# A transformer layer on one core: parameter loads, zero stores, the last head's output and the w_ada sums moved between stages

## The chip, the cores and the metric

The kernel runs on one core of a Trainium2 chip. The metric is the device time of one execution in microseconds (us). Five engines work side by side, each on its own queue in order: PE (matmuls), VectorE (DVE in the profile), ScalarE (ACT), GpSimd (POOL) and SP, which here only issues DMAs.

## The reference

One layer over 1024 latent tokens (plus 256 context tokens), all in float32, D = 1024:

```python
mod = silu(c) @ w_ada + b_ada                 # six vectors: shift, scale, gate, twice
h   = modulate(rmsnorm(x), sh1, sc1)          # context likewise, with c_ctx
q, k, v, z, xbc, dt_raw, gates = split(h @ w_in)
o   = differential attention, 8 heads, softmax(q1 k1) - lam * softmax(q2 k2), then rmsnorm per head
dt  = softplus(dt_raw + dt_bias); a = -exp(a_log)
y   = bidirectional state-space scan of silu(conv(xbc)) with dt, a  + d_skip * x
mix = (sigmoid(g_a) * (o @ w_branch_attn) + sigmoid(g_s) * (norm(y * silu(z)) @ w_branch_ssd)) @ w_out
x   = x + gt1 * rmsnorm(mix)
h   = modulate(rmsnorm(x), sh2, sc2)
f   = shared expert(h) + sum over the 8 chosen of 64 experts
out = x + gt2 * rmsnorm(f)
```

## The kernel before

The program is one class, `Layer`, whose stages follow one another: `norm_and_qkv`, `mixer_t`, `attention`, `merge_and_out`, `moe`, `final`. A product of two float32 matrices is made from three matmuls of high and low parts (`mm3`, L418): each operand is split on the way in, `hi` by a ScalarE copy and `lo` by a VectorE subtraction.

The order on PE, VectorE, ScalarE and GpSimd is written by a planner, `Flow` (L106). Each piece of work is a generator (a stream) that yields what it needs next: tiles, free buffers of a `Ring`, times, or an engine. `Flow.run` (L331) keeps a clock per engine from modelled durations and always continues the stream that can go first, the lowest priority number first; the instruction is emitted at that place. Where a yield holds a number, the stream goes on no earlier than that modelled time. On the chip the four engines then run their lists in that order, each waiting for its data. SP's list is not among those: `run` (L2420) hands only four engines over for a schedule by hand, and the framework orders SP's issues itself.

The places that the change touches:

- `ada_late` (L1508) computes 4096 of the modulation's columns while the q, k and v blocks run. For each of 32 columns of 128, a 512-KB chunk of w_ada comes into one of two `wada` buffers, VectorE sums its eight rows of c-weighted values into a `wacc` accumulator (L1538 to 1540), and PE adds over the partitions with a product with ones into the bank `adab` (L1545). One stream does the columns one after the other; two accumulators take turns.
- `mixer_ahead` (L763) opens the pool `tw` with the mixer's weight buffers during the last q block and starts the load of the dt weights. `mixer_t` (L784) loads `dcol` (d_skip) and `db` (dt_bias, a_log) at L813 to 818, in the pool `sp`, whose memory the buffers of the q, k and v blocks held before. `dt_post` (L826) is the first to need `db`: ScalarE takes its exponential, copies the three banks of dt products into `G` buffers (a ring of two), and PE folds them with 20 small matmuls.
- `branches` (L1194) multiplies the scan's and then the attention's output with their branch weights: four passes, (ssd, 0), (ssd, 1), (attn, 0), (attn, 1), each over half of the tokens, with 8 rows of outputs of 24 matmuls. `operands` (L1225) loads eight operands per pass, each 256 KB read back from DRAM, into `bxh` and `bxl`, rings of eight pairs, which one pass fills wholly: a pair comes free while the last row of the pass runs. All loads of this stage share four `braw` buffers.
- `norm` (L1470) in `attention` scales a finished head in the SBUF tile `ot` and stores it to DRAM (`oT`). Attention ends in the planner when eight heads are counted (L1505), and only then does the program go on to `merge_and_out`.
- `merge_and_out` (L1578) first fills a tile with zeros and stores it 16 times (256 KB each) over `yacc[1]` (L1603), to which half of the experts' outputs are added later; then w_out's 16 loads come as a stream of low priority (L1607). The output projection `main` (L1632) runs over eight tiles of 128 tokens, 48 matmuls each.

Of the kernel before, what the change touches and what calls it, by code (L numbers as in the profile page):

```python
# [9 lines left out]
F32 = mybir.dt.float32  # L10
# [364 lines left out]
class Layer:  # L375
# [387 lines left out]
    def mixer_ahead(s):  # L763

        F = s.F
        wp = s.open("tw")
        s.mw = raws, his, los = s.ring(wp, [P, KC, P], "raw", 2), s.ring(wp, [P, KC, P], "hi", 2, F32R), s.ring(wp, [P, KC, P], "lo", 2, F32R)
        s.zgs = s.ring(wp, [P, 512], "zg", 2)
        s.mbox = []
        F.spawn(0, s.mixer_load(COL_DT, 32, s.mbox))  # L770

    def mixer_load(s, c0, n, box):
# [11 lines left out]
    def mixer_t(s):  # L784
# [10 lines left out]
        if True:  # L795
# [14 lines left out]
            Rs = s.ring(sp, [P, 512], "R", 6)  # L810
            Gs = s.ring(sp, [P, 4, P], "G", 2)
            Ws = s.ring(sp, [P, 4, P], "W", 2)
            dcol = mp.tile([P, 8], F32, name="dcol")  # L813
            for q in range(2):
                F.dma(dcol[64 * q:64 * q + 64], bass.AP(tensor=I["d_skip"].tensor, offset=q, ap=[[0, 64], [2, 8]]))
            db = mp.tile([P, 2, 32], F32, name="db")
            F.dma(db[:, 0], s.brow("dt_bias", 0, 32))
            F.dma(db[:, 1], s.brow("a_log", 0, 32))
            dtn = mp.tile([P, 2, 10, 32], F32, name="dtn")
            dt, dtd = dtn[:, 0], dtn[:, 1]  # L820
            ac = mp.tile([P, 2, 10, 16], F32, name="ac")
# [372 lines left out]
    def branches(s):  # L1194


        F, I = s.F, s.I
        op, pp = s.open("fl", side="right"), s.open("fps", True, side="right")
        s.ysg = [s.dram(f"ysg{m}", [P, T]) for m in range(8)]
        s.oT = [s.dram(f"oT{h}", [P, T]) for h in range(8)]  # L1200
        s.acc = acc = s.ring(pp, [P, 512], "bacc", 2)
        s.raws = raws = s.ring(op, [P, 512], "braw", 4)
        xhs, xls = s.ring(op, [P, 512], "bxh", 8, F32R), s.ring(op, [P, 512], "bxl", 8, F32R)
        whs, wls = s.ring(op, [P, 4, P], "bwh", 3, F32R), s.ring(op, [P, 4, P], "bwl", 3, F32R)
        s.bxs = xs = {}
        ws = {}
        s.st = st = {"heads": 0, "pairs": 0, "merged": 0, "mg": None}
        todo = [("ssd", 0), ("ssd", 1), ("attn", 0), ("attn", 1)]

        def half(raw, hi, lo, then, first=False):  # L1210
            yield [raw, "ACT"]
            F.acopy(hi, raw)
            if first:
                yield [hi, "POOL"]
                F.ptt(lo, raw, hi.bitcast(F32), ALU.subtract)
            elif 0 < st["pairs"] < 32:
                yield [hi, "DVE"]
                F.tt(lo, raw, hi.bitcast(F32), ALU.subtract)
            else:
                yield [hi, "DVE|POOL"]  # L1220
                F.sub(lo, raw, hi.bitcast(F32))
            raws.put(raw)
            then()

        def operands():  # L1225
            for kind, h in todo:
                for k in range(8):
                    src = (s.yn if kind == "ssd" else s.oT)[k]
                    yield [raws, xhs, xls, "NOW"] + ([lambda: st["heads"] > k, src] if kind == "attn" else [])
                    raw, hi, lo = raws.get(), xhs.get(), xls.get()  # L1230
                    F.dma(raw, src[:, h * 512:h * 512 + 512])
                    F.spawn(3, half(raw, hi, lo, lambda q=(kind, h, k), v=(hi, lo): xs.update({q: v}), (kind, h, k) == todo[0] + (4,)))

        def weights():
            for kind, h in todo:
                wb = I["w_branch_" + kind][0].rearrange("(k p) c -> p k c", p=P)
                for m in range(8):
                    for a in range(2):
                        yield [raws, whs, wls, "NOW"]
                        raw, hi, lo = raws.get(), whs.get(), wls.get()  # L1240
                        rv = raw.rearrange("p (k c) -> p k c", k=4)
                        F.dma(rv, wb[:, 4 * a:4 * a + 4, m * P:(m + 1) * P])
                        F.spawn(3, half(rv, hi, lo, lambda q=(kind, h, m, a), v=(hi, lo): ws.update({q: v})))

        def main():
            for n, (kind, h) in enumerate(todo):
                for m in range(8):
                    if kind == "ssd":
                        yield [lambda: st["pairs"] >= PACE[8 * n + m]]
                    yield [acc]  # L1250
                    b = acc.get()
                    for k in range(KC):
                        yield [lambda: (kind, h, k) in xs and (kind, h, m, k // 4) in ws]
                        (xh, xl), (wh, wl) = xs[kind, h, k], ws[kind, h, m, k // 4]
                        yield [xh, F.ready[_n(xl)] + SLACK[5], wh, wl]
                        s.mm3(b, wh[:, k % 4], wl[:, k % 4], xh, xl, k == 0, k == KC - 1)
                        if k % 4 == 3:
                            whs.put(wh)
                            wls.put(wl)
                        if m == 7:  # L1260
                            xhs.put(xh)
                            xls.put(xl)
                    F.spawn(3, (gated if kind == "ssd" else merge)(h, m, b))

        def gated(h, m, b):
            sl = slice(h * 512, h * 512 + 512)
            yield [raws, "NOW"]
            g = raws.get()
            F.dma(g, s.gt[8 + m][:, sl])
            yield [g, b, "DVE"]  # L1270
            F.tt(g, b, g, ALU.mult)
            acc.put(b)
            F.dma(s.ysg[m][:, sl], g)
            raws.put(g)

        def merge(h, m, b):
            sl = slice(h * 512, h * 512 + 512)
            yield [lambda: st["mg"] is not None]
            ys, gs = st["mg"]
            yield [ys, gs, "NOW"]  # L1280
            y, g = ys.get(), gs.get()
            F.dma(g, s.gt[m][:, sl])
            F.dma(y, s.ysg[m][:, sl])
            yield [g, b, "DVE"]
            F.tt(g, b, g, ALU.mult)
            acc.put(b)
            yield [y, g, "DVE|POOL"]
            F.either(y, y, g, ALU.add)
            gs.put(g)
            yield [y, "ACT"]  # L1290
            hi, lo = s.mh[m, h], s.ml[m, h]
            F.acopy(hi, y)
            yield [hi, "DVE|POOL"]
            F.sub(lo, y, hi.bitcast(F32))
            ys.put(y)
            st["merged"] += 1

        F.spawn(3, weights())
        F.spawn(3, operands())
        F.spawn(4, main())  # L1300

# [37 lines left out]
    def attention(s):  # L1339
        tc, nc, F = s.tc, s.nc, s.F  # L1340
        ap, pp = s.open("at"), s.open("aps", True)
        if True:
# [127 lines left out]
            def norm(h, ot, s0):  # L1470
# [18 lines left out]
                for half in range(2):  # L1489
                    sl = slice(half * 512, half * 512 + 512)  # L1490
                    yield [F.ready[_n(r)] + SLACK[3], acc]
                    pb = acc.get()
                    for i in range(4):
                        F.tp(pb[:, i * P:(i + 1) * P], r[:, 4 * half + i:4 * half + i + 1].to_broadcast([P, P]), s.ident)
                    yield [pb, "DVE"]
                    F.stt(ot[:, sl], ot[:, sl], s.gsub, pb, ALU.mult, ALU.mult)
                    acc.put(pb)
                s0s.put(s0)
                F.dma(s.oT[h], ot)
                ots.put(ot)  # L1500
# [7 lines left out]
    def ada_late(s, pool, pm):  # L1508
# [3 lines left out]
        s.adar = s.dram("adar", [32, P])  # L1512
        wada = I["w_ada"][0].rearrange("(p k) c -> p k c", p=P)
        ws = s.ring(pool, [P, KC, P], "wada", 2)
        accs = s.ring(pool, [P, P], "wacc", 2)
        v = pool.tile([56, P], F32, name="lrows")
        F.dma(v[:32], bass.AP(tensor=I["b_ada"].tensor, offset=2048, ap=[[P, 32], [1, P]]))
        for i, n in enumerate(("g_post_mix", "g_pre_ffn", "g_post_ffn")):
# [5 lines left out]
        def loads():  # L1524
            for j in range(32):
# [3 lines left out]
                F.dma(w, wada[:, :, c0:c0 + P])  # L1529
                got.append(w)  # L1530

        F.spawn(0, loads())
        for j in range(32):
            yield [lambda: len(got) > 0]
            w = got.pop(0)
            yield [w, accs, "DVE"]
            acc = accs.get()
            F.ts(acc, w[:, 0], s.cc[:, 0, 0:1], None, ALU.mult)  # L1538
            for k in range(1, KC):
                F.stt(acc, w[:, k], s.cc[:, k, 0:1], acc, ALU.mult, ALU.add)  # L1540
                if k == 3:
                    yield ["DVE"]
            ws.put(w)
            yield [acc]
            F.mm(pm[:, j:j + 1], acc, s.ones[:, :1], True, True)  # L1545
            accs.put(acc)
        yield [v]
        F.tp(pm[:, 64:120], v, s.ident[:56, :56])
        yield [pm, "DVE"]
        F.vcopy(col, pm[:, 64:120])  # L1550
# [27 lines left out]
    def merge_and_out(s):  # L1578
# [21 lines left out]
        got = []  # L1600
        zero = pg.tile([P, 512], F32, name="zero")
        F.fill(zero, 0.0)
        for t in range(8):  # L1603
            for h in range(2):
                F.dma(s.yacc[1][t * P:(t + 1) * P, h * 512:(h + 1) * 512], zero)

        def weights():  # L1607
            for k in range(8):
# [23 lines left out]
        def main():  # L1632
            for t in range(8):
                tok = slice((t % 4) * P, (t % 4 + 1) * P)
                acc = accs[t % 2]
                yield [(acc, 2)]
                banks = [acc.get(), acc.get()]
                for k in range(KC):
# [825 lines left out]
```

## Time and profile before

| | us |
|---|---|
| median of three runs | 2836.93 |
| lowest and highest run | 2828.54, 2843.67 |
| the profiled execution | 2838.21 |
| its span, first to last instruction | 2836.1 |

| engine | busy us | share of the span |
|---|---|---|
| PE | 2624.0 | 93% |
| VectorE | 2000.2 | 71% |
| ScalarE | 1339.9 | 47% |
| GpSimd | 882.9 | 31% |

The shares are averages over stages with different limits, so they are read stage by stage: the q, k and v blocks end near 411 us, the mixer near 1050, attention near 1523, the merge and output projection near 1780, and the experts fill the rest up to the final 56 us. The mean granted clock of PE was 0.967 of the full 2.4 GHz. A row's "[idle before <- releaser]" is how long that engine stood before the instruction and what let it go; L163 is ScalarE's copy, L170 VectorE's two-tensor operation, L147 the matmul, L211 any DMA issued by SP.

### The profile page before, as it was taken

Reading aid. Unit: us, or ns where it says so; the run is one execution under the profiler, and the core shown is the slowest. Engines: PE = TensorE matmul, PEld = TensorE weight load, DVE = VectorE, ACT = ScalarE, POOL = GpSimd, SP = SyncE. Lnnn points to the kernel's source line nnn. Section 1 sums busy time; section 2 is a strip of 40 time slices with the busy share of each in tenths; the row PEclk is TensorE's granted clock in tenths of the full one; section 3 lists DMA queues with packets and bytes.
Section 4 is the critical chain, followed back from the end, with each engine's and each line's share of the span. In section 5 each row is a group of like instructions: output and inputs, shape, how many; then the busy total and the mean of one; then the engine's idle time right before and its main releaser. Section 6 shows DMA issues by size and latency. Waiting matters only on the chain. (4 is left out here: it accounts for less than half of the span.)

```text
span 2836.1 us, 41280 instructions
## 1 busy us (share of the span) xinstructions
PE 2624.0 (93%) x14561; PEld 2109.4 (74%) x14561; DVE 2000.2 (71%) x4690; ACT 1339.9 (47%) x2105; POOL 882.9 (31%) x670
## 2 busy tenths in 40 slices
PE   7999979999999999999998899899999998999991
PEld 4777868878787776888887687678887776777660
DVE  6876123577776658888893657867788877787863
ACT  4211113344444445666673422335666656576641
POOL 0101010444454520000000000056656656666641
PEclk9999989999999999999999999999999999999995
DMA  7667242243424345224234853478899998999997
GB/s 278 211 205 201 84 127 84 75 130 93 134 82 138 101 133 183 88 84 145 92 101 152 266 164 109 184 247 250 278 310 302 316 302 266 308 305 312 327 306 212
DMA packets 275266, 544.89 MB, mean 192 GB/s; under 512 B 31546, under 2 KB 166819, under 8 KB 248050
## 3 DMA queue, kind: packets, MB, share of 16 engines
q1 hardware_dynamic: 238898, 435.31, 45.1%
q0 software_dynamic: 36160, 106.93, 14.8%
q8 instruction: 115, 1.88, 0.3%
q14 instruction: 93, 0.76, 0.1%
HBM read 432.99 MB, written 124.73 MB: 197 GB/s over the span
## 5 line engine op out<-in xcount | busy, mean ns | idle before, releaser
L170 DVE TENSOR_TENSOR gl<-raw,gh 128x1024 fp32r<-128x1024 f32 x240 | 288.3, 1218 | 40.4 <-ACT gh L163 40.2
L147 PE MATMUL acc<-hh,hi 128*128 128x512 f32 (+2 forms) x760 | 303.7, 400 | 1.4 <-DVE ux L186 1.4
L163 ACT CAST gh<-raw 128x1024 fp32r<-128x1024 f32 x240 | 247.6, 1051 | 101.2 <-PE gu L147 65.9
L147 PE MATMUL acc<-hl,hi 128*128 128x512 f32 (+2 forms) x760 | 287.8, 379 | 0.0
L147 PE MATMUL gu<-gh,xh 128*128 128x512 f32 (+3 forms) x672 | 280.7, 418 | 3.8 <-ACT xh L163 3.4
L147 PE MATMUL acc<-hh,lo 128*128 128x512 f32 (+1 forms) x736 | 279.3, 380 | 2.5 <-DVE lo L170 2.5
L147 PE MATMUL gu<-gl,xh 128*128 128x512 f32 (+3 forms) x672 | 266.7, 397 | 4.4 <-DVE gl L170 4.3
L147 PE MATMUL gu<-gh,xl 128*128 128x512 f32 (+3 forms) x672 | 266.9, 397 | 3.8 <-DVE xl L170 3.7
L261 POOL DMA_INDIRECT cr<-cumd,crow x98 | 124.8, 1273 | 440.7 <-DVE y L197 408.8
L192 DVE TENSOR_SCALAR_CACHE_REDUCE e<-sps 128x512 f32<-128x512 f32 (+1 forms) x384 | 214.2, 596 | 31.2 <-PE sps L147 31.0
L267 POOL DMA_INDIRECT yacc<-y,tk x98 | 180.4, 1841 | 86.3 <-issue 31.3
L147 PE MATMUL sps<-qk 128*128 128x512 f32 (+1 forms) x768 | 195.4, 385 | 8.2 <-DVE e L192 4.5
L155 ACT ACTIVATE e<-e,st 128x1280 f32<-128x1280 f32 x128 | 174.7, 1366 | 31.2 <-DVE st L201 31.0
L147 PE MATMUL acc<-hi,hh 128*128 128x512 f32 x448 | 183.3, 409 | 0.0
L261 POOL DMA_INDIRECT wc<-wtab,tk x98 | 137.9, 1407 | 141.3 <-DVE tk L181 93.9
L147 PE MATMUL acc<-hi,hl 128*128 128x512 f32 x448 | 177.3, 396 | 0.4 <-DVE hl L170 0.4
L147 PE MATMUL acc<-lo,hh 128*128 128x512 f32 x448 | 177.1, 395 | 0.0
L147 PEld LDWEIGHTS sps<-qk 128*128 128x128 f32 x768 | 140.0, 190 | 41.7 <-DVE e L192 10.8
L147 PEld LDWEIGHTS acc<-hh,hi 128*128 128x128 f32 (+1 forms) x760 | 143.5, 189 | 31.2 <-issue 3.7
L147 PE MATMUL pv<-wr,vv 128*128 128x256 f32 x640 | 164.2, 380 | 0.0
L147 PEld LDWEIGHTS acc<-hl,hi 128*128 128x128 f32 (+1 forms) x760 | 143.7, 189 | 25.3 <-issue 0.6
L147 PEld LDWEIGHTS acc<-hh,lo 128*128 128x128 f32 x736 | 139.6, 190 | 29.7 <-DVE lo L170 3.0
(323 smaller groups left out, 6253.7 us busy)
## 6 DMA issues: line engine op xcount, KB each, us to landing
raw<-in_w_e_gate_dram SPq DMA_DIRECT2D x64, 1024.0 KB, 10.6
raw<-in_w_e_up_dram SPq DMA_DIRECT2D x64, 1024.0 KB, 11.3
draw<-in_w_e_down_dram SPq DMA_DIRECT2D x64, 1024.0 KB, 10.0
qk<-qk POOLq DMA_DIRECT2D x16, 1664.0 KB, 8.4
raw<-in_w_in_dram SPq DMA_DIRECT2D x40, 512.0 KB, 4.6
wada<-in_w_ada_dram SPq DMA_DIRECT2D x32, 512.0 KB, 5.2
R<-acd SPq DMA_DIRECT2D x64, 256.0 KB, 5.4
qk<-sa SPq DMA_DIRECT2D x52, 256.0 KB, 4.3
```

What stands on the lines that cost most here:

```text
L147: s.nc.tensor.matmul(out, l, r, start=start, stop=stop)
L155: s.nc.scalar.activation(out, in_, fn, **kw)
L163: s.nc.scalar.copy(out, in_)
L170: s.nc.vector.tensor_tensor(out, a, b, op=op)
L192: s.nc.vector.tensor_scalar(out, a, s1, None, op0=op0, op1=op1, accum_out=acc)
L261: s.nc.gpsimd.indirect_dma_start(out=out, out_offset=None, in_=table, in_offset=bass.IndirectOffsetOnAxis(ap=idx, axis=0), **kw)
L267: s.nc.gpsimd.indirect_dma_start(out=table, out_offset=bass.IndirectOffsetOnAxis(ap=idx, axis=0), in_=in_, in_offset=None, compute_op=ALU. ...
```

## The change

Four edits, all of order and place; no product or sum is added or left out.

1. `dcol` and `db` become tiles of the pool `tw`, and their four loads are issued in `mixer_ahead`, before the load of the dt weights.
2. In `ada_late` a column's VectorE work is planned 4 us after its chunk is expected, and its matmul becomes a stream of its own, planned 4 us after the sum is expected; four accumulators instead of two.
3. The 16 zero stores are emitted in the output projection's loop, two in front of each tile's matmuls.
4. The first half of head 7's output is split from SBUF inside `norm`, into a pair of `branches`' rings, and `operands` no longer loads it.

```diff
@@ mixer_ahead
+        s.dcol, s.db = wp.tile([P, 8], F32, name="dcol"), wp.tile([P, 2, 32], F32, name="db")
+        F.dma(s.db[:, 0], s.brow("dt_bias", 0, 32))
+        F.dma(s.db[:, 1], s.brow("a_log", 0, 32))
+        for q in range(2):
+            F.dma(s.dcol[64 * q:64 * q + 64], bass.AP(tensor=s.I["d_skip"].tensor, offset=q, ap=[[0, 64], [2, 8]]))
         F.spawn(0, s.mixer_load(COL_DT, 32, s.mbox))
@@ mixer_t
-            dcol = mp.tile([P, 8], F32, name="dcol")
-            for q in range(2):
-                F.dma(dcol[64 * q:64 * q + 64], bass.AP(tensor=I["d_skip"].tensor, offset=q, ap=[[0, 64], [2, 8]]))
-            db = mp.tile([P, 2, 32], F32, name="db")
-            F.dma(db[:, 0], s.brow("dt_bias", 0, 32))
-            F.dma(db[:, 1], s.brow("a_log", 0, 32))
+            dcol, db = s.dcol, s.db
@@ branches, operands
+                    if (kind, h, k) == ("attn", 0, 7):
+                        yield [lambda: ("attn", 0, 7) in xs]
+                        continue
@@ attention, norm
                     acc.put(pb)
+                    if (h, half) == (7, 0):
+                        yield [*s.bx, ot, "ACT"]
+                        hi, lo = (q.get() for q in s.bx)
+                        F.acopy(hi, ot[:, sl])
+                        yield [hi, "DVE"]
+                        F.tt(lo, ot[:, sl], hi.bitcast(F32), ALU.subtract)
+                        s.bxs["attn", 0, 7] = hi, lo
@@ ada_late
-        accs = s.ring(pool, [P, P], "wacc", 2)
+        accs = s.ring(pool, [P, P], "wacc", 4)
+        def column(j, acc):
+            yield [F.ready[_n(acc)] + 4000.0]
+            F.mm(pm[:, j:j + 1], acc, s.ones[:, :1], True, True)
+            accs.put(acc)
+            done.append(j)
-            yield [w, accs, "DVE"]
+            yield [F.ready[_n(w)] + 4000.0, accs, "DVE"]
             ws.put(w)
-            yield [acc]
-            F.mm(pm[:, j:j + 1], acc, s.ones[:, :1], True, True)
-            accs.put(acc)
-        yield [v]
+            F.spawn(0, column(j, acc))
+        yield [v, lambda: len(done) == 32]
@@ merge_and_out
-        for t in range(8):
-            for h in range(2):
-                F.dma(s.yacc[1][t * P:(t + 1) * P, h * 512:(h + 1) * 512], zero)
             for t in range(8):
                 tok = slice((t % 4) * P, (t % 4 + 1) * P)
                 acc = accs[t % 2]
+                for h in range(2):
+                    F.dma(s.yacc[1][tok.start + t // 4 * 512:tok.stop + t // 4 * 512, h * 512:(h + 1) * 512], zero)
                 yield [(acc, 2)]
```

## Rows read from the trace of the kernel before

**Rows 1.** Stretches (us): PE, PEld, DVE, ACT, POOL busy, clock, DMA share, GB/s

```profile
60.00:260.00 200.00, 189.93 (x890) 155.12 (x891) 161.83 (x372) 40.45 (x58) 25.23 (x18) 0.97 0.70 208
...
411.50:424.00 12.50, 0.04 (x1) 0.04 (x1) 0.00 (x0) 0.79 (x3) 0.00 (x0) 0.60 0.19 40
...
435.00:1050.00 615.00, 588.53 (x3358) 491.41 (x3357) 407.84 (x962) 260.50 (x373) 244.12 (x208) 0.98 0.35 106
...
1544.80:1555.80 11.00, 0.00 (x0) 0.00 (x0) 0.00 (x1) 0.62 (x1) 0.00 (x0) 0.61 1.03 356
...
1555.80:1582.00 26.20, 21.13 (x67) 14.38 (x68) 14.46 (x22) 11.15 (x18) 0.00 (x0) 0.84 0.80 252
...
1582.00:1620.00 38.00, 38.00 (x169) 31.32 (x167) 30.50 (x48) 18.74 (x32) 0.00 (x0) 1.00 0.86 271
...
1664.00:1770.00 106.00, 106.00 (x527) 85.54 (x526) 69.23 (x208) 26.77 (x61) 0.00 (x0) 1.00 0.32 112
...
1770.00:2780.00 1010.00, 955.16 (x5813) 732.79 (x5812) 785.42 (x1516) 582.60 (x912) 566.98 (x392) 0.98 0.88 285
```

**Rows 2.** Waits of PE, 0 to 410 us: total, times, longest

```profile
PE adab L147 <- DVE wacc L186: 7.9, 3, 4.7
```

**Rows 3.** Timeline of PE, 140 to 158: start, length, operation [idle before]

```profile
149.70 0.59 PE L147 MATMUL adab<-cst,wacc 128*128 128x1 f32 x2 [4.66 <-DVE wacc L186]
...
150.15 0.77 PE L147 MATMUL acc<-hi,hh 128*128 128x512 f32 x1
...
154.13 0.56 PE L147 MATMUL acc<-hi,hh 128*128 128x512 f32 x1
```

**Rows 4.** Timeline of VectorE (DVE), 136 to 158

```profile
146.64 0.29 DVE L179 TENSOR_SCALAR wacc<-wada,cc 128x128 f32<-128x128 f32 x1 [6.70 <-DMA wada<-in_w_ada_dram]
```

**Rows 5.** Timeline of SP's DMA issues, 285 to 500

```profile
345.35 4.34 SPq L211 DMA_DIRECT2D raw<-in_w_in_dram  x3
...
405.00 3.79 SPq L211 DMA_DIRECT2D qk<-sb  x4
...
409.99 1.78 SPq L211 DMA_DIRECT2D dcol<-in_d_skip_dram  x2
...
412.76 0.43 SPq L211 DMA_DIRECT2D db<-in_a_log_dram  x1
```

**Rows 6.** Timeline of ScalarE (ACT), 335 to 432

```profile
423.21 0.23 ACT L155 ACTIVATE db<-db 128x32 f32<-128x32 f32 x1 [19.21 <-DMA db<-in_a_log_dram]
```

**Rows 7.** Timeline of PE, 424 to 437

```profile
423.96 4.47 PE L147 MATMUL aux<-fold,G 64*128 64x32 f32 x20 [12.48 <-ACT G L163]
...
428.37 0.79 PE L147 MATMUL acc<-hh,hi 128*128 128x512 f32 x1
...
434.08 0.54 PE L147 MATMUL acc<-hl,hi 128*128 128x512 f32 x1
```

**Rows 8.** Timeline of SP's DMA issues, 1470 to 1660

```profile
1540.49 9.39 SPq L211 DMA_DIRECT2D yacc<-zero  x13
...
1550.68 0.58 SPq L211 DMA_DIRECT2D braw<-in_w_branch_ssd_dram  x1
...
1630.24 0.33 SPq L211 DMA_DIRECT2D braw<-in_w_out_dram  x1
```

**Rows 9.** Timeline of PE, 1544 to 1572

```profile
1555.82 0.80 PE L147 MATMUL bacc<-bxh,bwh 128*128 128x512 f32 x1 [11.03 <-ACT bwh L163]
...
1560.25 0.63 PE L147 MATMUL bacc<-bxl,bwh 128*128 128x512 f32 x1
...
1570.15 0.50 PE L147 MATMUL bacc<-bxh,bwh 128*128 128x512 f32 x1 [2.84 <-ACT bxh L163]
```

**Rows 10.** Stretch 415 to 417, columns as in rows 1

```profile
415.00:417.00 2.00, 0.00 (x0) 0.00 (x0) 0.00 (x0) 0.00 (x0) 0.00 (x0) 0.50 0.05 0
```

**Rows 11.** Tile wacc: lengths in ns, first and last start

```profile
L179 DVE TENSOR_SCALAR wacc<-wada,cc x32: 273/285/1320, 84.0 to 247.2; 128x128 f32<-128x128 f32 x32
```

**Rows 12.** Tile woh: lengths in ns, first and last start

```profile
L147 PE MATMUL gu<-woh,mh x64: 389/389/499, 1669.0 to 1761.6; 128*128 128x512 f32 x64
```

More of the change, by code (lines that the diff above doesn't have):

```diff
@@ L1202, in branches @@
         s.raws = raws = s.ring(op, [P, 512], "braw", 4)
-        xhs, xls = s.ring(op, [P, 512], "bxh", 8, F32R), s.ring(op, [P, 512], "bxl", 8, F32R)
+        s.bx = xhs, xls = s.ring(op, [P, 512], "bxh", 8, F32R), s.ring(op, [P, 512], "bxl", 8, F32R)
         whs, wls = s.ring(op, [P, 4, P], "bwh", 3, F32R), s.ring(op, [P, 4, P], "bwl", 3, F32R)
@@ L1530, in loads @@
                 got.append(w)
+        def column(j, acc):
[3 more added lines that the diff above has]
+            done.append(j)
+        done = []
         F.spawn(0, loads())
```

## The prediction

> **What bounds the kernel now.** I read the stretches first [rows 1]: PE's busy time, its granted clock and the DMA share, stage by stage. PE is busy over 94% of the long stretches, in one fixed order of instructions. So the kernel is as long as PE's work plus PE's gaps, and a gap that closes moves everything behind it forward. Three dents are to be seen: 60 to 260 us (189.93 busy of 200), 411.5 to 424 (0.04 of 12.5) and 1544.8 to 1555.8 (nothing of 11, while the DMA share is 1.03). I then asked for PE's waits and followed each dent back on the engine that released it.
>
> The first dent: PE waited three times, 7.9 us in all, for the w_ada sums `wacc` [rows 2], the longest 4.66 us [rows 3]. VectorE itself had stood 6.70 us for the chunk `wada` from DMA [rows 4]. A late load blocks VectorE's queue, and VectorE's late sum blocks PE's.
>
> The second dent: SP issued `dcol` and `db` at 410 to 413 us, behind the last `qk` stores [rows 5]. ScalarE stood 19.21 us until `db` had landed [rows 6]. Its next instructions are the copies of the dt banks, PE's fold matmuls need these and waited 12.48 us, and the first conv matmuls stand behind the folds in PE's order [rows 7].
>
> The third: SP issued 13 of the 16 zero stores from 1540.49 on, one per 9.39/13 = 0.72 us, and the next chunk of w_branch_ssd only at 1550.68 [rows 8]. PE waited 11.03 us for its split [rows 9].
>
> Each dent also drops the clock to the lower level (1.2 GHz): the 14 matmuls from 428.37 to 434.08 stand 0.44 us apart [rows 7], against 38.00/169 = 0.225 at the full level [rows 1]. A slow matmul costs about 0.21 us more.
>
> **1, parameters ahead.** Nothing is added; four issues move from 410 to about 345 us, beside the first mixer weights (the three `raw` loads at 345.35 [rows 5]). Gone: the 12.48 us wait; 14 x 0.21 = 3.0 us of slow conv matmuls; and about half of the 4.47 us of folds, 2.2 us, an estimate from the two clock levels. Kept: the third dt copy, which needs a G buffer back from PE; 1 us is my estimate, from its neighbours' lengths. Sum 16.7, taken as 16. Bounds 12 (the wait alone) to 17.7. Where it shifts, the dt chain and all loads tied to it shift along; the mixer's PE (588.53 of 615 busy) has 4% of waits that move as they are.
>
> The cost at the new place: SP spends some 3 us on four issues. Behind them stands the load of the dt weights, wanted by PE only after the last `qk` block, whose stores run to 405 [rows 5]. At 415 to 417 us the DMA share was 0.05 with nothing else running [rows 10]: the scattered parameters went through about one engine of 16 (0.8 of one) until 423. So up to 10 us of one engine now lie ahead of a share of the dt weights, and ScalarE, which splits them, can stand for as long. PE's cover is the accumulator ring of four banks, some 5 us of matmuls each (24 x 0.225). I take 0; with the cover gone it is 10 us once.
> The Trainium skill would price this differently ("DMA: Bandwidth & Descriptors", the section on why a DMA increments its semaphore by 16): the engine count is the largest divisor up to 16 of the slowest dimension, which for 64 partitions means all 16 engines. By that rule the 10 us bound would be under 1 us. The row speaks for one engine, and the bound stays at 10.
>
> **2, w_ada's sums.** The instructions stay; the planner now places VectorE's chain 4 us after it thinks the chunk landed and PE's matmul 4 us after it thinks the sum is done, with four accumulators instead of two. Against the late load of 6.70 us there are 8 us in series for PE. Gone: 7.9 us of waits; after the longest, ten matmuls from 150.15 to 154.13 were slow [rows 3], 2.1 us, and the other waits' share goes by their length, 2.1 x 3.2/4.66 = 1.4. Sum 11.4; taken as 10, since VectorE's 4 us cover less than 6.70 and what stands behind it there are the rope steps that PE needs. Bounds 4.7 (the longest wait alone) to 11.4. Later sums cost nothing: the last started at 247 us [rows 11], and only the end of the `qk` blocks near 400 waits for them. Even 4 us on each of 32 columns, unhidden, ends at 247 + 128 = 375.
>
> **3, zeros and the last head.** Gone from the dent: 11.03 us, and eleven slow matmuls (1555.82 to 1560.25 [rows 9]) x 0.21 = 2.3; 13.3 in all. SP issues the same 16 stores later. In the out-projection (1664 to 1770) the share is 0.32 and 16 x 0.72 = 11.5 us of transfers would hide. But does SP leave them there? Its queue is not written by hand, the other engines' are. The loads of conv weights come from a later stage of the program than the `qk` stores, and the trace has them before those stores (345.35 against 405.00 [rows 5]): what has its data and its memory ready goes up. A zero store needs only the memset. So it probably leaves soon after it, between the loads of the merge, where the share is 0.80 and then 0.86 [rows 1]. There 26.2 x 0.20 + 38 x 0.14 = 10.6 us are free over 64 us: hidden only if the stores are spread. Bounds: 0 kept (a block of 11.5 us again, now before the attention operands) to 13.3. I take 7, the middle, because both bounds rest on rows of equal weight.
> The last head: one ScalarE copy and one VectorE subtraction move from the read-back to the norm; one 256-KB load of 16 (0.72 us) goes. PE waited 2.84 us at 1570.15 for such operands; I take 1, bounds 0 and 2.8. The added wait: head 7's norm now waits for an operand pair, and none is free before the last ssd row's first product (24 products, 5.4 us of PE, before the attention rows begin). Behind it stand the second half of the norm, its store, and, because the planner closes attention on the eighth head, all of the out stage: the memset, w_out's loads, the merge buffers. Its cover is large: the last w_out load left at 1630.24 [rows 8] and the first out-projection matmul ran at 1669.0 [rows 12]. Price 0; without cover it is the hold itself, some 13 us.
>
> **Sum.** 16 + 10 + 7 + 1 = 34 us. The profiled execution took 2838.2 us (2.1 beside its span); it would be 2804. It stands 1.3 above the median of 2836.9, so I forecast 2803. All upper bounds: 17.7 + 11.4 + 13.3 + 2.8 = 45, 2792; all lower: 12 + 4.7 = 17, 2820.
>
> **Rivals.**
> *The zeros don't move.* The change then doesn't do what it says: SP takes all 16 as a block right after the later memset, just when the attention operands are wanted. For it: the conv loads that went up, and nothing that a zero store waits for. Against it: once loads compete they come earlier in the program. Price: 7 us back, 2810. Chance 0.25. The Trainium skill ("DMA: Bandwidth & Descriptors", "Issuing engines are not separate DMA queues") has all transfers interleave on the same 16 engines; by that a spread of the stores doesn't empty the merge either. The share of 1.03 under the block agrees.
> *The mixer keeps A's wait.* The planner could still put the dt copies late or the unit chain could pace the mixer, so part 1 gives only 4: 2815. Against: the copies stood behind one instruction alone, and that for its load [rows 6]. Chance 0.1.
> *The waits only change names.* VectorE's rope steps, the attention operands and w_out's loads take up what is freed; under 14 us are left, 2825 to 2840. Chance 0.09.
> *Slower: the planner's order of the experts.* All of PE's order comes from the planner's clock, which these edits shift. In 1770 to 2780 PE is busy 955.16 of 1010, with a DMA share of 0.88; the 55 us of gaps come from close meetings of weight splits and loads. If a new order makes these gaps over 34 us longer, the gain is gone; doubled, they give 2803 + 55 = 2858. For: little slack at 0.88. Against: experts start from the same routing, with the same rings. Chance 0.04.
>
> **Numbers.** The forecast case has 0.52, from 2792 to 2814. To it come the first two rivals, which are faster too: 0.87 for faster by over 0.5% (14 us, about what a measurement of this kernel can tell from no change), 0.09 within, 0.04 slower. The range runs from 2789 (all upper bounds and a little of the runs' own spread of 8 us) to 2821 (all lower bounds).
>
> **What would show it.** Right: the fold matmuls run at once after the dt matmuls at full clock, `db` lands near 350; PE's waits for `wacc` are under 1 us; no 11-us wait before the last ssd rows; the read-back loads of head outputs count 15. The place of the `zero` stores on SP, before or after the first out-projection matmul, decides part 3. Wrong: a new PE wait of 10 us at the start of the attention products or at 350; PE reaching the first expert less than 20 us earlier; or an expert stretch longer than 1010 us by over 10.

## The result and the profile after

The changed kernel took 2798.27 us (median of 4 runs, 2792.73 to 2803.03) against 2833.86 us before in the same comparison: ratio 0.9862, 95% interval 0.984 to 0.9884, so 1.4% faster. The forecast was 2803 us, with a range of 2789 to 2821. The profiled execution took 2803.03 us with a span of 2801.1 (before 2838.21 and 2836.1): 35.0 us of span went. The total was right; what follows shows that not all of its terms were.

First the stretches of the changed kernel (start:end, length, busy time of PE, PEld, DVE, ACT, POOL, clock, DMA share, GB/s), beside [rows 1].

```profile
60.00:260.00 200.00, 197.85 (x950) 162.92 (x951) 165.14 (x362) 41.73 (x61) 29.09 (x20) 1.00 0.71 215
389.90:401.00 11.10, 11.10 (x53) 6.96 (x50) 1.38 (x2) 2.68 (x4) 0.00 (x0) 0.85 0.71 190
1500.30:1633.50 133.20, 123.44 (x527) 97.28 (x526) 83.39 (x135) 52.90 (x89) 1.42 (x1) 0.97 0.79 253
1628.00:1734.00 106.00, 106.00 (x527) 85.60 (x526) 69.47 (x207) 26.27 (x61) 0.00 (x0) 1.00 0.32 113
1734.00:2744.00 1010.00, 955.43 (x5817) 734.03 (x5814) 785.39 (x1516) 583.92 (x912) 570.14 (x392) 0.98 0.88 285
```

All three dents of [rows 1] are gone: PE works 197.85 of the 200 us from 60 to 260, runs straight from the first DT matmul at 390.0 to the folds at 401.0, and has no 11-us hole in the merge. The out-projection and the experts are what they were. The same stretch of the merge in the kernel before, from the end of the last pv matmul to the first out-projection matmul, reads:

```profile
1522.70:1669.00 146.30, 126.41 (x526) 99.35 (x526) 83.33 (x136) 53.71 (x89) 0.00 (x0) 0.92 0.73 232
```

So the merge lost 13.1 us: 10.1 of idle PE (19.9 against 9.8) and 3.0 of matmuls at the lower clock. The next table follows PE through four places, in us from the start of the span, for all kernels of this study (the timeline of PE; the parts are numbered as in the prediction, 4 being the last head, which stood there in part 3).

| kernel | first conv matmul | last pv ends | out-projection starts | pv to out-projection | ratio to before, interval |
|---|---|---|---|---|---|
| before | 428.4 | 1522.7 | 1669.0 | 146.2 | 1 |
| part 1 alone | 416.8 | 1512.6 | 1660.7 | 148.1 | 0.997, 0.9955 to 0.9984 |
| part 2 alone | 416.2 | 1508.9 | 1659.2 | 150.3 | 0.995, 0.9933 to 0.9968 |
| part 3 alone | 429.4 | 1526.5 | 1666.0 | 139.5 | 0.9971, 0.9956 to 0.9987 |
| part 4 alone | 430.7 | 1525.8 | 1670.4 | 144.6 | 0.9984, 0.9966 to 1.0001 |
| after (all four) | 403.3 | 1500.3 | 1633.5 | 133.1 | 0.9862, 0.984 to 0.9884 |
| without part 4 | 405.5 | 1499.4 | 1640.2 | 140.8 | 0.9899, 0.9882 to 0.9915 |
| hold alone for part 4 | 403.3 | 1501.3 | 1636.3 | 134.9 | 0.9875, 0.9858 to 0.9891 |
| without part 4, w_out held | 405.5 | 1500.0 | 1634.2 | 134.2 | 0.9861, 0.9839 to 0.9884 |
| dcol behind DT weights | 402.3 | 1499.4 | 1632.4 | 132.9 | 0.9882, 0.9862 to 0.9902 |
| zeros late | 404.6 | 1499.3 | 1630.9 | 131.6 | 0.9859, 0.9843 to 0.9876 |
| both of these | 401.0 | 1499.8 | 1630.7 | 130.9 | 0.9841, 0.9819 to 0.9864 |

The medians of before in these comparisons were 2834 to 2848 us, so only ratios and stretches are compared across them. The expectations below count the last stretch from the start of the last printed row of pv (149.1 before, 133.7 after); that row merges four or twelve matmuls, so the table takes its end. The places of a kernel are those of one execution, and they scatter: the stretch from pv to the out-projection takes 146.2, 148.1 and 150.3 in the three kernels that lack parts 3 and 4, and 133.1 and 132.9 in two others whose merge is the same. A difference of under 2 us between two kernels is therefore not shown by them alone.

### The profile page after: what moved, and what is told of

The parts are those of the page before. It is cut to its first block, busy times and chain, and to the rows that moved or that the text cites. A ratio compares the mean times of both kernels' runs of the same rounds, so it can differ in the third digit from the quotient of the medians.

```text
span 2801.1 us, 41274 instructions
## 1 busy us (share of the span) xinstructions
PE 2618.4 (93%) x14561; PEld 2101.6 (75%) x14561; DVE 2008.3 (72%) x4690; ACT 1339.9 (48%) x2104; POOL 888.9 (32%) x671
## 3 DMA queue, kind: packets, MB, share of 16 engines
q0 software_dynamic: 36160, 106.93, 15.1%
## 5 line engine op out<-in xcount | busy, mean ns | idle before, releaser
L261 POOL DMA_INDIRECT cr<-cumd,crow x98 | 118.9, 1213 | 312.5 <-DVE crow L186 280.9
L261 POOL DMA_INDIRECT wc<-wtab,tk x98 | 143.7, 1466 | 137.7 <-DVE tk L181 101.1
## 6 DMA issues: line engine op xcount, KB each, us to landing
raw<-in_w_e_up_dram SPq DMA_DIRECT2D x64, 1024.0 KB, 12.4
```

Source lines behind the costliest of these rows:

```text
L261: s.nc.gpsimd.indirect_dma_start(out=out, out_offset=None, in_=table, in_offset=bass.IndirectOffsetOnAxis(ap=idx, axis=0), **kw)
```

## The experiments

**Each part alone.** The edits are the four parts of the diff, one at a time on the kernel before.

Part 1:

```
+        s.dcol, s.db = wp.tile([P, 8], F32, name="dcol"), wp.tile([P, 2, 32], F32, name="db")
...
-            dcol = mp.tile([P, 8], F32, name="dcol")
```

> The kernel before with part 1 alone (dcol and db loaded in mixer_ahead). Read by leads against the profile of the kernel before: the first DT matmul must not move (lead 0), the first convolution matmul shows the wait that went. Theory 1 (each part is worth what its own stretch shows): lead 14 us at the first convolution matmul, 11 to 14 at the end, since the changed kernel lost about 3 us of its lead inside the mixer; time 11 to 14 us below before. Theory 2 (the terms as predicted): 16 at the spot and at the end. Theory 3 (the ScalarE wait for the DT weights, 9 us in the changed kernel, costs when the late sums no longer hide it): the lead is under 8 us.

Part 2:

```
-            yield [w, accs, "DVE"]
+            yield [F.ready[_n(w)] + 4000.0, accs, "DVE"]
...
+            F.spawn(0, column(j, acc))
```

> The kernel before with part 2 alone (4 us of slack and an own stream for the sums of w_ada, four accumulators). Theory 1: lead 10 to 11 us at the first DT matmul, and the lead stays up to the end, so 10 to 11 us less time; TensorE's waits for wacc go from 7.9 to under 1 us. Theory 2: the lead is given back at dcol and db, which are loaded late as before and are issued by an order that does not follow the matmuls: lead 10 at the first DT matmul, under 4 at the first convolution matmul and at the end.

Part 3:

```
-                F.dma(s.yacc[1][t * P:(t + 1) * P, h * 512:(h + 1) * 512], zero)
...
+                    F.dma(s.yacc[1][tok.start + t // 4 * 512:tok.stop + t // 4 * 512, h * 512:(h + 1) * 512], zero)
```

> The kernel before with part 3 alone (the zero stores stand in the loop of the out-projection; the last head goes through DRAM as before). Theory 1 (the 16 stores ahead of the ssd weights are the whole wait of 11 us): the wait before the last ssd rows goes, lead at the first out-projection matmul 11 to 13 us, time 11 to 13 us less, as with parts 3 and 4 together. Theory 2 (the stores come between the merge's loads and give part of it back, as predicted): 5 to 8 us. Theory 3 (the parts need each other): under 4 us alone.

Part 4:

```
+                    if (kind, h, k) == ("attn", 0, 7):
...
+                        yield [*s.bx, ot, "ACT"]
```

> The kernel before with part 4 alone (the first half of the last head split from SBUF; the zero stores stand at the start of the merge as before). Theory 1 (the held stream also delays the memset and the stores behind it by some 16 us, so that the ssd weights and the first attention operands are issued ahead of them): the 11-us wait before the last ssd rows is gone with the stores untouched, lead at the first out-projection matmul 8 to 13 us, and so parts 3 and 4 do not add. Theory 2 (part 4 as predicted, worth the waits at the end of the first merge pass alone): 0 to 2.8 us, and the wait of 11 us stands. Theory 3 (the hold costs): slower by up to 13 us.

Measured: 0.3%, 0.5%, 0.29% and 0.16% faster; the interval of part 4 reaches 1.0001, so its gain is not told from none. The four ratios multiply to 0.9876, against 0.9862 for all. The 0.3% of part 1 are 8.5 us (4.6 to 12.8 by the interval), less than the 11 to 14 of its theory 1. In the places of the table, part 1 brings the first conv matmul forward by 12.7 us (429.5, the mean of the three kernels that lack parts 1 and 2, less 416.8), part 2 by 13.3. On top of the other they do nearly the same, 11.8 and 12.4 (404.4, the mean of the five kernels with both parts unaltered, against 416.2 and 416.8). Part 1 alone was to leave the first DT matmul where it was. It comes 2.2 us later: 318.8 us after VectorE's first w_ada sum, against 316.2 to 316.8 in the three kernels without parts 1 and 2, and PE waits once more for `r`, 2.4 us (more on this below). At the first conv matmul part 1 is a little under the 14 of theory 1, under the 16 of theory 2 and well over theory 3, and part 2's lead is not given back at the mixer's parameters; it is even larger than theory 1's 10 to 11.

In the merge part 3 alone reaches 139.5 us, where the three kernels without parts 3 and 4 take 148.2 on average: 8.7, give or take the 2 us of their scatter. That lies between the two theories; the 11-us wait is gone, but waits for other loads remain. Part 4 alone gives 3.6 us, which is hardly more than that scatter (1.6 us against the kernel before), and its trace shows theory 1 half right: the held stream does let the ssd weights pass, and the stores then stop the attention operands. Its SP timeline, and behind it PE's:

```profile
1555.24 0.32 SPq L211 DMA_DIRECT2D oT<-ot  x1
1555.78 2.38 SPq L211 DMA_DIRECT2D yacc<-zero  x3
1560.43 8.96 SPq L211 DMA_DIRECT2D yacc<-zero  x13
1570.17 1.72 SPq L211 DMA_DIRECT2D braw<-oT  x3
```

```profile
1575.29 0.80 PE L147 MATMUL bacc<-bxh,bwh 128*128 128x512 f32 x1 [11.98 <-ACT bxh L163]
```

The last operands leave after all 16 stores, and PE waits 11.98 us for their split, as it did 11.03 for the weights in [rows 9]. None of the three theories came whole: the old wait went, as in theory 1, but not the 8 to 13 us; and neither the stretch nor the time excludes the 0 to 2.8 us of theory 2.

**What does part 4 add beside part 3?** By stretches parts 3 and 4 give 8.7 and 3.6 alone and 15.1 together (148.2 less 133.1), so part 4 seems worth more once the zeros are gone: 7.7 (140.8 less 133.1). The times agree (0.9899 without it, 0.9862 with it). Two kernels take part 4 apart.

```
-                    if (kind, h, k) == ("attn", 0, 7):
...
-                        hi, lo = (q.get() for q in s.bx)
-                        F.acopy(hi, ot[:, sl])
```

The kernel without part 4 lacks it whole; the one of this edit keeps only its wait line, and half 0 of the last head goes through DRAM again.

> The changed kernel without part 4: parts 1, 2 and 3, the last head through DRAM, nothing held. Read by the stretch from the last pv matmul of the attention to the first matmul of the out-projection: 149.1 us before, 133.7 in the changed kernel, 142.2 with part 3 alone. Theory 1 (part 4 is worth some 8 us once the zeros are gone): 140 to 143 us, and the time 8 us above the changed kernel, about 1.1% below before. Theory 2 (part 4 is worth 1 us, 2.8 at most, as predicted, and the rest is scatter of the runs): 134.5 to 136.5 us.

> The changed kernel with the wait of part 4 kept (the second half of the last head waits for a free buffer of each branch ring and for ScalarE) but without its split: the last head's first half goes through DRAM, as before. Theory 1 (what part 4 gives comes from the hold: the out-projection's loads start later, so the branch weights and operands go first): the stretch from the last pv matmul to the first matmul of the out-projection stays at 133 to 136 us. Theory 2 (it comes from the operands that no longer go through DRAM): 140 to 143 us. In between, 136 to 140: both.

Without part 4 the stretch is 140.8, with the hold alone 134.9, with all of it 133.1: the hold gives 5.9 of 7.7 us, the SBUF operands 1.8 (a size that single executions don't show for certain). So the added wait, which looked like a cost, is most of the gain. SP's timeline without part 4 shows what it keeps away:

```profile
1509.19 0.33 SPq L211 DMA_DIRECT2D braw<-in_w_out_dram  x1
...
1518.29 0.44 SPq L211 DMA_DIRECT2D braw<-in_w_out_dram  x1
...
1525.04 0.33 SPq L211 DMA_DIRECT2D braw<-in_w_out_dram  x1
...
1526.91 0.50 SPq L211 DMA_DIRECT2D braw<-oT  x1
```

Loads of w_out, wanted at 1640, leave before the first head output that the merge wants at once, and each takes one of the four `braw` buffers through which the branch weights and operands also pass. If that is the cause, holding w_out alone must do the same.

```
         def weights():
+            yield [lambda: ("attn", 0, 7) in s.bxs]
             for k in range(8):
```

> Parts 1, 2 and 3 without part 4 and without any hold, but with the loads of w_out not begun before the attention branch's last operand is split; TensorE's order is that of the kernel without part 4, whose stretch from the last pv matmul to the first out-projection matmul took 143.6 us. Theory 1 (the hold of part 4 helped because w_out's loads then no longer take the four braw buffers and the DMA queue from the branch weights and operands): 135 to 138 us, as with the hold alone (136.6). Theory 2 (the hold helped by the order of the other engines, or by the later stores, iota and router loads): 141 to 144 us. If w_out comes too late, TensorE waits for woh or wol at the first out-projection matmul, and the stretch is longer than 144.

It does. First SP's issues in this kernel, then PE's waits for the operands from 1500 to 1670 us, without the gate and with it (total, times, longest):

```profile
1523.38 0.80 SPq L211 DMA_DIRECT2D braw<-oT  x2
...
1539.96 0.33 SPq L211 DMA_DIRECT2D braw<-in_w_out_dram  x1
```

```profile
PE bacc L147 <- ACT bxh L163: 11.1, 7, 4.4
```

```profile
PE bacc L147 <- ACT bxh L163: 5.7, 5, 2.8
```

The stretch falls from 140.8 to 134.2 with nothing held in the norm, no operand taken from SBUF, and PE's order unchanged. Of the 6.6 us, 5.4 are these waits (PE's whole idle time fell by 5.0, 12.7 to 7.7), and 17.0 us at the lower clock became 13.7. The ratio is 0.9861, that of the whole change. So the place of w_out's loads is enough for nearly all of part 4's gain beside part 3.

What the loads hold up is not told apart so well. The gate moves their splits too, and in the kernel without part 4 ScalarE stands 2.51 us for the third w_out chunk ahead of its first split of a head output, which with the gate comes 5.5 us earlier (first without the gate, then with it):

```profile
1528.24 0.62 ACT L163 CAST woh<-braw 128x512 fp32r<-128x512 f32 x1 [2.51 <-DMA braw<-in_w_out_dram]
...
1532.15 0.62 ACT L163 CAST bxh<-braw 128x512 fp32r<-128x512 f32 x1
```

```profile
1526.63 0.62 ACT L163 CAST bxh<-braw 128x512 fp32r<-128x512 f32 x1 [1.31 <-DMA braw<-oT]
```

The first head output itself leaves 3.5 us earlier (1523.38 against 1526.91). How much falls to the buffers, to the DMA queue and to ScalarE's order no run separates, and 2.4 of the 5.4 us were waits near 1590, long after those early loads.

**Where do the zeros cost?** In the changed kernel the stores left 43 us after their memset (1529.9), in ones to threes between the loads of the merge, but all before the out-projection began at 1633.5. First and last of them on SP:

```profile
1573.20 0.90 SPq L211 DMA_DIRECT2D yacc<-zero  x2
...
1621.87 2.49 SPq L211 DMA_DIRECT2D yacc<-zero  x3
```

To force them into the out-projection, the memset was moved there, and the wait for free banks was put ahead of the stores.

```
-        F.fill(zero, 0.0)
...
+                yield [(acc, 2)]
+                if t == 0:
+                    F.fill(zero, 0.0)
...
-                yield [(acc, 2)]
```

> The changed kernel with the memset of the zeros put into the loop of the out-projection, behind its first wait for banks, so that no store of zeros can be issued before the out-projection runs; TensorE's order is the same. Theory 1 (the stores that the DMA queue issues between the merge's loads cost nothing there): the stretch from the last pv matmul to the first out-projection matmul stays at 133.7 us within 1, the time within 3 us of the changed kernel. Theory 2 (the 4 MB still give part of the gain back, as the prediction's term says): the stretch is 2 to 6 us shorter. Theory 3 (the stores then collide with the first experts' weights): the stretch of the experts is 2 to 6 us longer.

The stretch is 131.6 against 133.1 (with dcol moved as well, 130.9 against 132.9). By these two pairs the 4 MB between the loads cost some 1.5 to 2 us, just under theory 2 and over theory 1, and near the limit of what single executions show. In the first pair it is not waiting that went (9.6 us idle against 9.8) but work at the lower clock:

```profile
1499.30:1630.90 131.60, 122.00 (x526) 96.55 (x525) 82.69 (x135) 53.05 (x89) 0.00 (x0) 0.99 0.72 224
```

Theory 3 stays open. From the first to the last hT matmul of the experts this kernel takes 958.5 us and the changed one 965.0, but over the twelve kernels this stretch runs from 955.3 to 976.2, and it is 975.2 in the other kernel with late zeros, so 2 to 6 us can't be seen there. The time (0.9859 against 0.9862) shows no loss.

**What did part 1 cost at its new place?** The changed kernel's SP queue, ScalarE, PE and VectorE near 340:

```profile
332.82 0.44 SPq L211 DMA_DIRECT2D db<-in_a_log_dram  x1
333.30 1.31 SPq L211 DMA_DIRECT2D dcol<-in_d_skip_dram  x2
334.65 0.62 SPq L211 DMA_DIRECT2D raw<-in_w_in_dram  x1
...
338.18 1.03 SPq L211 DMA_DIRECT2D raw<-in_w_in_dram  x1
```

```profile
346.64 0.50 ACT L163 CAST hi<-raw 128x128 fp32r<-128x128 f32 x2 [9.25 <-DMA raw<-in_w_in_dram]
...
392.17 0.23 ACT L155 ACTIVATE db<-db 128x32 f32<-128x32 f32 x1
```

```profile
350.22 0.66 PE L151 MATMUL tr<-cst,r 128*128 128x128 f32 x4 [2.30 <-POOL r L174]
...
401.00 2.41 PE L147 MATMUL aux<-fold,G 64*128 64x32 f32 x20
```

```profile
346.97 0.49 DVE L170 TENSOR_TENSOR hi<-raw,hi 128x128 fp32r<-128x128 f32 x2 [57.87 <-ACT hi L163]
347.38 0.69 DVE L170 TENSOR_TENSOR ra<-acc,rope 128x512 f32<-128x512 f32 x1
```

The DT weights, issued right behind dcol, keep ScalarE waiting 9.25 us (part 2 alone, without the parameters there: 3.51). VectorE's half of that split stands behind it, the rope steps of the qk blocks behind that, and PE waits 2.30 us for `r`, a wait that the kernel before does not have. The test puts dcol behind the DT weights:

```
-        for q in range(2):
-            F.dma(s.dcol[64 * q:64 * q + 64], bass.AP(tensor=s.I["d_skip"].tensor, offset=q, ap=[[0, 64], [2, 8]]))
...
         F.dma(raw[:, :, :n], s.I["w_in"][0].rearrange("(k p) c -> p k c", p=P)[:, :, c0:c0 + n])
+        if n == 32:
+            for q in range(2):
+                F.dma(s.dcol[64 * q:64 * q + 64], bass.AP(tensor=s.I["d_skip"].tensor, offset=q, ap=[[0, 64], [2, 8]]))
```

> The changed kernel with the two dcol loads issued behind the load of the DT weights instead of ahead of it; TensorE's order is the same. Theory 1 (dcol's packets delay the DT weights by 6 us, ScalarE and, behind its split, VectorE stand, and TensorE waits 2.3 us for r near 350): that wait goes, ScalarE waits about 3.5 us for the DT weights instead of 9.25, the first DT matmul comes 2.3 us earlier than in the changed kernel, measured from the first qkv matmuls, and 2 us of it are left at the end (under what the times can tell). Theory 2 (the wait has another cause): no change at the first DT matmul.

PE's waits of 300 to 395 us, after and with dcol behind:

```profile
PE tr L151 <- POOL r L174: 4.8, 2, 2.5
```

```profile
PE tr L151 <- POOL r L174: 2.5, 1, 2.5
```

The wait is gone, and from VectorE's first w_ada sum on the first DT matmul comes after 301.5 us instead of 303.9. The four other kernels with dcol ahead and part 2 take 303.6 to 305.6, part 2 alone 301.1. Theory 1 holds, and the gain, as expected, is too small for the times (0.9882 against 0.9862, the intervals overlap).

**Both together**, as a candidate:

> The changed kernel with dcol loaded behind the DT weights and the memset of the zeros inside the out-projection, the two edits that took a wait away or cost nothing when tried singly; TensorE's order is the same. Expected of both theories: 2 to 3 us less than the changed kernel (2.3 us near 350, 0 to 1 us at the merge), a ratio of 0.985 to 0.986 against before. It would be wrong if the two together lose the gain of either: first DT matmul not 2 us earlier from the first sums of w_ada on, or the stretch before the out-projection over 136 us.

301.0 us to the first DT matmul, 130.9 in the merge, ratio 0.9841: better than 0.985 to 0.986 at the median and the lowest ratio of the study, but its interval, 0.9819 to 0.9864, holds the changed kernel's 0.9862. The traces show it faster by some 5 us in these two places (2.9 and 2.2); the times can't tell.

## Why the prediction was right or wrong

**Part 1 (16 taken, 12 to 17.7): 12 to 13.** The wait of 12.48 us went whole, and the folds fell from 4.47 to 2.41 us, as worked out. Two terms failed. One is the cost at the new place, "I take 0": it was 2.30 us of PE, by the very path that was named (the dt weights late, ScalarE standing) and one that was not (VectorE's queue behind ScalarE's split). The accumulator ring did not cover it, since PE wanted `r`, not a bank. The other is the 3.0 us of slow conv matmuls: PE's clock is at its lower level from 403.8 to 407.2 in the changed kernel too, across the first conv matmuls, and PE has two short waits there. The first eighteen of them take 7.0 us before and, with one short pair of matmuls between them, 7.0 us after (first before, then after; the row behind the eighteenth closes each):

```profile
428.37 0.79 PE L147 MATMUL acc<-hh,hi 128*128 128x512 f32 x1
...
435.39 0.43 PE L147 MATMUL aux<-dtn,cst 128*128 128x160 f32 x2
```

```profile
403.34 0.50 PE L147 MATMUL acc<-hh,hi 128*128 128x512 f32 x1
...
410.37 0.43 PE L147 MATMUL aux<-dtn,cst 128*128 128x160 f32 x2
```

What is left, 12.48 + 2.06 - 2.30 = 12.2, is what was measured.

The reading "about one engine of 16" was not sound. The share of 0.05 is a mean over sixteen engines, and a twentieth of each gives it as well as 0.8 of one. In the changed kernel's trace the completion of each of the two dcol loads comes in sixteen steps, spread from 339.94 to 341.01 and from 344.78 to 346.00 us, as that of the 128 KB of DT weights does (345.40 to 346.61), which speaks for all sixteen. So does the Trainium skill's rule ("DMA: Bandwidth & Descriptors", the section on why a DMA increments its semaphore by 16), by which 64 partitions mean 16 engines. But the estimate of under 1 us that the prediction worked out from this rule was wrong: the loads landed 7.7 and 12.0 us after their issue.

**Part 2 (10 taken, 4.7 to 11.4): 12 to 13.** All 7.9 us of waits for `wacc` went. Whether the 4 us of slack on each side did it, the stream of its own or the two more accumulators, no run tells apart. From 80 to 260 us, first before, then with part 2 alone:

```profile
80.00:260.00 180.00, 170.07 (x784) 138.26 (x783) 144.06 (x341) 30.49 (x43) 22.59 (x16) 0.97 0.75 224
```

```profile
80.00:260.00 180.00, 178.31 (x845) 146.30 (x843) 147.79 (x331) 31.70 (x45) 26.46 (x18) 1.00 0.76 231
```

PE's idle time fell from 9.93 to 1.69 us, by 8.2, and 7.9 of it are the waits. Slow matmuls come on top of that. The ten behind the longest wait cost 2.1 us, as worked out; behind the wait of 2.01 us that ends at 215.74, eight more take 3.45 us (kernel before):

```profile
216.04 0.78 PE L147 MATMUL acc<-hi,hh 128*128 128x512 f32 x1
...
219.49 0.39 PE L147 MATMUL acc<-hi,hl 128*128 128x512 f32 x1
```

At 0.225 each they would take 1.8, so some 1.6 us are lost there; behind the third wait, of 1.19 us up to 111.93, the clock stayed at 1.00. Together that is 8.2 + 2.1 + 1.6 = 11.9 us, near the 11.4 that the prediction had added up (it gave both smaller waits 1.4). The step that failed is the cut from 11.4 to 10, because VectorE's 4 us would cover less than the 6.70: no wait for `wacc` was left. What is measured above 11.9 lies within the scatter of the places, 428.4 to 430.7 in the three kernels without parts 1 and 2.

**Part 3 (7 taken, 0 to 13.3): 8.7 alone and 7.4 beside parts 1 and 2 (148.2 less 140.8), for another reason than given.** The wait of 11.03 us and its slow matmuls went as worked out. The prediction gave half of it back because the zeros would leave "soon after" the memset. They did go up ahead of the out-projection, but 43 us after it (24 and 26 us in the two kernels with part 3 and nothing held) and spread, at a price of some 1.5 to 2 us. What kept the rest was w_out. Its early loads were no new thing: in the kernel before, too, three of them leave ahead of the first head output, at the sides of the block of zeros.

```profile
1532.51 0.33 SPq L211 DMA_DIRECT2D braw<-in_w_out_dram  x1
...
1553.70 0.33 SPq L211 DMA_DIRECT2D braw<-in_w_out_dram  x1
...
1558.05 0.33 SPq L211 DMA_DIRECT2D braw<-in_w_out_dram  x1
...
1561.38 0.32 SPq L211 DMA_DIRECT2D braw<-oT  x1
```

When the zeros went, three stayed in front (above), and holding w_out's loads gave 6.6 us more. "The waits only change names" had w_out's loads on its list, and got a chance of 0.09 for a far larger sum.

**Last head (1 taken, 0 to 2.8): 3.6 alone, 7.7 beside part 3.** The operands from SBUF, priced at 1 with a bound of 2.8, gave some 1.8. The failed step is the added wait: "Price 0; without cover it is the hold itself, some 13 us." Only losses were looked for. The prediction had listed w_out's loads among what stands behind the hold, and known 39 us of slack for them ([rows 8] against [rows 12]); it did not ask whom they had been in the way of.

**Sum.** By the two profiled executions the lead was 25.0 us at the first conv matmul (26 forecast for parts 1 and 2, 3.0 of it just behind that matmul), fell by 2.6 up to the last pv (0 forecast), rose by 13.1 in the merge (8 forecast) and fell by 0.5 behind it: 35.0 against 34. The errors of parts 1 and 2 cancel, and those of the merge and of the stretch before it nearly do. So the waits that go were read rightly, but that their sum came out within 1 us is luck. The 2.6 us are open: from the first conv matmul to the end of pv the twelve kernels take 1092.7 to 1098.8 us, before 1094.3 and after 1097.0, and no part goes with it.

**The rivals.** The zeros left neither in a block after the memset nor in the out-projection: the first rival's place was half right, its price not. The mixer did not keep the wait. The experts' stretch kept its length in the two profiled executions, 955.16 and 955.43 us busy of 1010 (965.7 and 965.0 us from the first to the last hT matmul), so no cost of the planner's new order is seen there, beside a scatter of 21 us over all kernels.

## What to carry to other kernels

A wait added to a stream is also a delay of all that this stream would have issued; if those issues share a buffer ring or a queue with work that is wanted sooner, and have slack of their own, the delay is a gain and deserves a price with either sign. When a block of transfers is moved away, look at what else stands in front of the wanted loads: here w_out's early loads kept back 6.6 of 14.0 us (148.2 less 134.2), and one line that holds them did nearly as much as the whole of part 4. And of a small load that is moved ahead, follow the next load in the queue, the engine that waits for it, and the engines that wait behind that one.

## What was not expected of the hardware

Two loads of 2 KB, written as 64 rows of eight separate four-byte elements, held up everything behind them. In the changed kernel the DT weights (128 KB) were issued at 334.65, a store of 256 KB at 337.41 and a further load of 512 KB at 338.18, and yet from 340 to 344 us the rate was 0 GB/s (stretches of the changed kernel, columns as above):

```profile
340.00:342.00 2.00, 2.00 (x10) 1.59 (x10) 0.00 (x0) 0.00 (x0) 0.00 (x0) 1.00 0.05 0
342.00:344.00 2.00, 2.00 (x10) 1.61 (x9) 0.00 (x0) 0.00 (x0) 0.00 (x0) 1.00 0.05 0
344.00:346.00 2.00, 2.00 (x10) 1.61 (x9) 0.00 (x0) 0.00 (x0) 0.00 (x0) 1.00 0.69 159
```

The share of 0.05 is that of [rows 10], but there nothing else was wanted. Here two loads and a store stood in the same queue; the rate rose to 159 GB/s from 344 us on, between dcol's two landings (341.0 and 346.0). The kernel with dcol behind the DT weights shows it again: it issued a store at 339.02 and 512 KB at 339.40, and moved 0 GB/s from 340 to 344. The prediction had reckoned with a load on one engine beside which the other fifteen go on. Why the queue stood as a whole no run here tells apart.
